# Decode attention with queries and probabilities as 32-column weights and the cache as the moving operand

## The chip, the cores and the metric

The kernel runs on one core of one Trainium2 chip. The metric is the device time of one execution in microseconds. Before the change it is 2065.58 us (median of 3 runs, 2065.29 to 2065.72).

The core has five engines that work side by side, each through its own instructions in order: TensorE (PE; its weight loads are listed apart as PEld), VectorE (DVE), ScalarE (ACT), GpSimd (POOL) and SyncE (SP), which here issues DMAs. TensorE multiplies a stationary operand (the weights, at most 128 rows by 128 columns) with a moving operand and writes to PSUM. The number of weight columns is the number of output partitions, and the number of moving columns is the length of the output.

## The reference

One layer of a hybrid decoder runs for a prompt of 256 tokens and for 8 decode sequences of one token each: a SwiGLU feed-forward half step, a mixing stage in which one half of the width is attention (16 query heads of 64, 4 key/value heads, window 128, a sink per head) and the other half an RWKV-7 recurrence, an output projection, a second SwiGLU, and norms. Everything is float32. The part in question is the attention of the decode tokens:

```python
def swa_decode(q, k, v, k_buf, v_buf, rel_bias, sinks):
    kc = jnp.concatenate([k_buf, k], axis=1)      # 128 cached keys and the token's own
    vc = jnp.concatenate([v_buf, v], axis=1)
    ...
    s = einsum('...qhgd,...khd->...hgqk', q, kc) * HEAD_DIM ** -0.5 + bias
    m = maximum(max(s), sink)
    p = exp(s - m);  denom = sum(p) + exp(sink - m)
    o = einsum('...hgqk,...khd->...qhgd', p / denom, vc)
```

So there are 8 sequences x 16 heads = 128 rows of 129 scores, and 128 output rows of 64. Each sequence has its own cache of 128 x 256 keys and as many values; a key/value head serves 4 query heads.

## The kernel before

**Layout and order.** All activations are held transposed: features on the partitions, and 264 columns for the 256 prompt tokens and the 8 decode tokens, so prompt and decode go through the large products together. Weights stream in chunks of 128 x 512: SP issues the load (tile `raw`), ACT rounds it to a high part (`hi`), VectorE takes the rest (`lo`), and each 128 x 128 piece costs three fast products (`gemm`, `chunk`, `mm`, line 73). The stages in time: first feed-forward, mixing from about 790 us, output projection from about 1160, second feed-forward from about 1300.

**Mixing as tasks.** `mixing_body` computes one tile of projected columns after another (`SEQ`: RWKV batches, then keys and values, then eight query tiles). What follows from a tile is a generator: `prep` and `chain` for RWKV, `kvtask` for keys and values, `attend` for one pair of query heads of the prompt, `dec_attend` for the decode tokens, `dec_state` for the RWKV state of the decode tokens. After every weight chunk `tick` lets each task go on to its next `yield`. That gives the order in the program; a planner with its own model of time then orders the instructions of each engine, and hands out buffers. Temporaries come from a pool of `NT` = 25 tiles (`tmp`, named `t` in the profile), loaded blocks from a ring of `NLD` = 6 (`load`, named `ld`), which bias, cached keys, cached values and state blocks share. A load waits on the SP queue until its buffer is free, and weight loads come behind it on that queue.

**Output projection.** It runs in three passes over the inner dimension (`PASS`): first the 8 RWKV tiles, then 6 attention tiles, then 2. The attention tasks run on during the first pass; the second needs them finished (`need`, `drain`), the decode part included: its results are copied into columns 256 to 263 of the attention tiles (line 813) and only then split into `hi` and `lo` (line 854).

**Decode attention before.** `attend` puts the 8 decode queries of its two heads into `qd` (line 708). `dec_attend` then

- spreads `qd` into `qb`, with zeros in the half of the partitions that belongs to the other head (line 756);
- for each of 2 pairs of key/value heads and 8 sequences loads the cached keys and multiplies with the keys as weights (128 x 128) and 8 query columns moving (line 765): 16 products, whose scores come out as positions by rows;
- copies the scores out, transposes them to rows by positions (line 773), computes the product with the token's own key separately (`pr` against `ones`), and adds bias, takes the softmax with the sink (`softmax`);
- transposes the probabilities back (line 787), spreads those of the token's own key with a diagonal matrix and a product with `ones`, and multiplies them with its own value on VectorE (`od`);
- multiplies the cached values as weights (128 x 128) with 8 probability columns moving: 16 products; adds them to `od`.

In the trace the 32 products with the cache are the rows `m<-t,ld`. Each float32 product is two instructions there.

Of the kernel before, what the change touches and what calls it, by code (L numbers as in the profile page):

```python
# [15 lines left out]
NB = 8  # L16
# [13 lines left out]
NS, NO, NH, NT, NLD = 45, 8, 40, 25, 6  # L30
# [13 lines left out]
CID, CBO, CCM, CTR, CMK = 0, 128, 256, 384, 512  # L44


def body(tc, I, O):
# [8 lines left out]
    def tt(e, out, a, b, op):  # L56
        return e.tensor_tensor(out=out, in0=a, in1=b, op=op)  # L57
# [36 lines left out]
    with ExitStack() as ctx:  # L94
# [48 lines left out]
        C = cp.tile([P, 640], F32, name="C")  # L143
# [146 lines left out]
        def mixing_body(mx, n2, n3):  # L290
            def fix(shape, name):
                return mx.tile(list(shape), F32, name=name)
# [4 lines left out]
            def load(src, shape):  # L297
                t = ring(shape, "ld", NLD)
                SP.dma_start(t, src)
                return t  # L300
# [16 lines left out]
            qd = fix((P, 2, NB, 4), "qd")  # L317
# [361 lines left out]
            def kvtask(w, p, x):  # L679
                A.dma_start(O[("kp", "vp")[w]][p], x[:, P:NP])  # L680
                yield
                tp = mp()
                TE.transpose(tp[0:8, 256:384], x[:, NP:T], ident)
# [21 lines left out]

            def attend(t, q):
                p = t // 4
                G.tensor_copy(qd[:, p, :, t % 4], q[:, NP:T])
# [41 lines left out]
            def dec_attend(att):  # L750
                yield
                qb = tmp((P, 2, NB, 2, 4))
                G.memset(qb, 0.0)
                for h in range(2):
                    r = HALF[h]
                    G.tensor_copy(qb[r, :, :, h, :], qd[r])
                yield
                sps = mp()
                sv = sps[:, :P].rearrange("p (h x) -> p h x", h=2)
                for p in range(2):  # L760
                    for b in range(0, NB, 2):
                        kc = load(I["kc"][p, b // 2], (P, 2, P))
                        for j in range(2):
                            c0 = p * 32 + (b + j) * 4
                            mm(sv[:, :, c0:c0 + 4], kc[:, j, :], qb[:, p, b + j])
                st = tmp((P, P))
                A.copy(st, sps[:, :P])
                pr = tmp((P, 2, NB, 4))
                for p in range(2):
                    tt(G, pr[:, p], qd[:, p], bc(kT[p][:, NP:T].unsqueeze(2), (P, NB, 4)), ALU.mult)  # L770
                yield
                s2 = mp()
                TE.transpose(s2[:, 0:P], st, ident)
                for h in range(2):
                    r = HALF[h]
                    mm(s2[r, P:P + 1], pr[r], ones[r, 0:1])
                bd = load(I["bd"], (P, 129))
                s = tmp((P, 129))
                mxv = ring((P, 2), "mxv", 6)
                V.tensor_tensor_reduce(out=s, in0=s2[:, 0:129], in1=bd, op0=ALU.add, op1=ALU.max, scale=1.0,  # L780
                                       scalar=vc(VSD), accum_out=mxv[:, 0:1])
# [6 lines left out]
                pt = tmp((P, P))  # L788
                A.copy(pt, tp[:, 0:P])
                pn = mp()  # L790
                for h in range(2):
                    r = HALF[h]
                    mm(pn[r, 0:64], ones[:, 0:64], dg[:, r])
                od = tmp((P, 2, NB, 4))
                for p in range(2):
# [4 lines left out]
                ov, pv = (x[:, :P].rearrange("p (h x) -> p h x", h=2) for x in (op, pt))  # L800
                for b in range(NB):
                    vcache = load(I["cv"][b], (P, 256))
                    for p in range(2):
                        c0 = p * 32 + b * 4
                        mm(ov[:, :, c0:c0 + 4], vcache[:, p * P:(p + 1) * P], pv[:, :, c0:c0 + 4])
                of = od.rearrange("p a b i -> p (a b i)")
                for h in range(2):
                    r = HALF[h]
                    tt(V, of[r], ov[r, h, :], of[r], ALU.add)
# [133 lines left out]
def layout(i):  # L943
# [3 lines left out]
    for n in (1, 2):  # L947
# [9 lines left out]
    heads = np.array([(2 * p + h) * 4 + j for h in range(2) for p in range(2) for b in range(NB) for j in range(4)])  # L957
# [9 lines left out]
                                 np.concatenate([m, m], 0)], 1).astype(f4))  # L967
# [46 lines left out]
```

## Time and profile before

| | |
|---|---|
| median of 3 runs | 2065.58 us |
| profiled execution, its own time | 2070.28 us |
| span of the profiled execution, first to last instruction | 2068.3 us |
| busy share PE / PEld / DVE / ACT / POOL | 97 / 95 / 63 / 51 / 14% |
| instructions | 45747 |
| mean granted TensorE clock | 0.99 |
| moved by DMA | 358.40 MB, mean 173 GB/s |

The profile is that of one execution. A row of the view by lines has the line of the kernel, the engine, the operation, what it writes and reads (buffer numbers left out), the shapes and the count; behind the bar stand the busy time in us, the mean time of one in ns, and the idle time of the engine before it with what ended it. Where a helper issues the instruction, its line is shown (73 for `mm`, 57 for `tt`), so the tile names tell the uses apart. A row of the timeline has start, length, engine, line, operation, tiles and count. A row of the view by stretches gives for each engine the busy time and, in brackets, the instructions. A row of the waits names the waiting engine and line, what it waited for, the time in total, how often, and the longest.

### The profile page before, as it was taken

To read this page: it belongs to the slowest core of one execution; us is meant where nothing else is said; L and a number is where in the kernel's file an instruction comes from. 1 tells how busy PE (TensorE), PEld (TensorE's weight loads), DVE (VectorE), ACT (ScalarE), POOL (GpSimd) and SP (SyncE) were. 2 spreads that over 40 slices of the span, in tenths; PEclk is the share of its full clock that TensorE was granted. 3 is DMA by queue.
4 is the path that set the end of the run, shared out by engine and by line. 5 is a ranking of instruction groups with operands and counts; after the bars stand their busy time and mean duration, and the time that the engine had idled before them with its cause. 6 is when DMAs were issued, how large, how long until landed. Compare 5 with 4: busy or idle time off the path is not lost.

```text
span 2068.3 us, 45747 instructions
## 1 busy us (share of the span) xinstructions
PE 2016.5 (97%) x17162; PEld 1973.1 (95%) x17162; DVE 1308.5 (63%) x2618; ACT 1056.2 (51%) x2080; POOL 287.9 (14%) x375
## 2 busy tenths in 40 slices
PE   8999999999999999989999899999999999999997
PEld 8999999999999999989998788999999999999997
DVE  5765555555555586668778788656555555655555
ACT  5644444444444466656565635544444444444445
POOL 0301001020110221211100052110101102010012
PEclk9999999999999999989999999999999999999998
DMA  6555565655555575443454465556555565555554
GB/s 225 176 177 185 175 206 177 195 179 176 186 174 188 181 217 188 140 121 104 143 144 129 125 183 180 177 181 181 181 175 186 169 193 181 179 182 176 185 174 139
DMA packets 228686, 358.40 MB, mean 173 GB/s; under 512 B 42304, under 2 KB 84304, under 8 KB 228432
## 3 DMA queue, kind: packets, MB, share of 16 engines
q1 hardware_dynamic: 222768, 346.82, 53.6%
q10 hardware_dynamic: 5696, 8.66, 1.1%
q8 instruction: 134, 2.20, 0.4%
q14 instruction: 88, 0.72, 0.1%
HBM read 347.25 MB, written 10.21 MB: 173 GB/s over the span
## 4 chain that ended last, share of the span: by engine, by line
PE 90%; DVE 4%; DMA 3%; issue 1%; ACT 1%; SPq 1%; POOL 0%; DVEq 0%; ACTq 0%; POOLq 0%
PE acc L73 82%; PE m L73 7%; DVE lo L57 1%; DMA raw<-in_gu 1%; DMA TT<-sb 1%; DMA sb<-Xt 1%; ACT L67 0%; DMA out_wkvs<-ld 0%; DVE s L60 0%; DVE s L57 0%; ACT t L67 0%; DVE ld L57 0%; DMA ld<-in_st 0%; SPq L509 0%; DVE y L57 0%
## 5 line engine op out<-in xcount | busy, mean ns | idle before, releaser
L73 PE MATMUL acc<-s,hi 128*128 128x264 f32 x6728 | 1257.8, 286 | 10.4 <-ACT hi L122 9.0
L57 DVE TENSOR_TENSOR lo<-raw,hi 128x512 fp32r<-128x512 f32 (+2 forms) x1304 | 877.3, 676 | 597.0 <-ACT hi L122 573.7
L122 ACT CAST hi<-raw 128x512 fp32r<-128x512 f32 (+2 forms) x1304 | 778.6, 602 | 880.2 <-PE acc L73 802.2
L73 PEld LDWEIGHTS acc<-s,hi 128*128 128x128 f32 x6728 | 1053.5, 190 | 18.4 <-ACT hi L122 10.3
L73 PE MATMUL acc<-s,lo 128*128 128x264 f32 x3364 | 964.3, 287 | 14.1 <-DVE lo L57 13.8
L73 PEld LDWEIGHTS acc<-s,lo 128*128 128x128 f32 x3364 | 636.0, 189 | 21.7 <-DVE lo L57 18.5
L73 PE MATMUL acc<-t,hi 128*128 128x264 f32 x2752 | 503.1, 285 | 1.6 <-ACT t L251 1.6
L73 PEld LDWEIGHTS acc<-t,hi 128*128 128x128 f32 x2752 | 426.1, 188 | 1.9 <-ACT t L251 1.8
L73 PE MATMUL acc<-t,lo 128*128 128x264 f32 x1376 | 388.5, 284 | 0.0
L57 POOL TENSOR_TENSOR t<-t,t 128x264 f32<-128x264 f32 (+1 forms) x146 | 156.8, 1074 | 1206.6 <-ACT hi L122 912.9
L73 PEld LDWEIGHTS acc<-t,lo 128*128 128x128 f32 x1376 | 258.3, 188 | 0.0
L57 DVE TENSOR_TENSOR t<-acc,t 128x264 f32<-128x264 f32 x164 | 70.9, 432 | 36.4 <-PE acc L73 36.1
L73 PE MATMUL acc<-o,hi 128*128 128x264 f32 x344 | 66.4, 284 | 0.0
L57 POOL TENSOR_TENSOR o<-o,o 128x264 f32<-128x264 f32 x48 | 40.7, 848 | 168.6 <-ACT o L67 166.2
L73 PEld LDWEIGHTS acc<-o,hi 128*128 128x128 f32 x344 | 53.3, 188 | 0.0
L67 ACT ACT_TABLE_LOAD x40 | 51.3, 1283 | 2.4 <-PEq L1006 1.2
L60 DVE SCALAR_TENSOR_TENSOR s<-acc,s 128x264 f32<-128x264 f32 x96 | 40.6, 427 | 16.8 <-PE acc L73 16.3
L73 PE MATMUL acc<-o,lo 128*128 128x264 f32 x172 | 49.1, 286 | 0.0
L60 DVE SCALAR_TENSOR_TENSOR x<-acc,x 128x264 f32<-128x264 f32 x96 | 40.5, 426 | 10.1 <-PE acc L73 9.7
L67 ACT ACTIVATE t<-t 128x264 f32<-128x264 f32 x94 | 40.0, 426 | 3.9 <-DVE t L57 2.4
L57 DVE TENSOR_TENSOR st<-X,Xt 128x60 f32<-128x60 f32 (+10 forms) x120 | 24.5, 204 | 22.3 <-DMA ld<-in_sT 9.7
L251 ACT CAST t<-t 128x264 fp32r<-128x264 f32 x86 | 35.5, 412 | 3.7 <-POOL t L57 2.3
(218 smaller groups left out, 1090.4 us busy)
## 6 DMA issues: line engine op xcount, KB each, us to landing
raw<-in_gu SPq DMA_DIRECT2D x688, 256.0 KB, 3.2
raw<-in_dn SPq DMA_DIRECT2D x224, 256.0 KB, 2.7
raw<-in_win SPq DMA_DIRECT2D x152, 256.0 KB, 3.3
raw<-in_dn SPq DMA_DIRECT2D x160, 192.0 KB, 2.7
raw<-in_wout SPq DMA_DIRECT2D x48, 256.0 KB, 3.5
raw<-in_wout SPq DMA_DIRECT2D x32, 128.0 KB, 2.5
xsp<-x ACTq DMA_DIRECT2D x16, 132.0 KB, 3.5
s<-xsp SPq DMA_DIRECT2D x16, 132.0 KB, 2.3
```

The lines of the kernel that those rows point to most:

```text
L57: return e.tensor_tensor(out=out, in0=a, in1=b, op=op)
L60: return V.scalar_tensor_tensor(out=out, in0=a, scalar=s, in1=b, op0=op0, op1=op1)
L67: return A.activation(out=out, in_=in_, func=f, **k)
L73: TE.matmul(out, lhsT, rhs, start=start, stop=stop, **k)
L122: A.copy(hi[:, :w], raw[:, :w])
L251: A.copy(hi, u)
```

## The change

The roles of the operands in the decode attention are exchanged. The queries, and later the probabilities, become weights of 32 columns, and the cached keys and values move.

- The 8 sequences are numbered b = 4u + g. Group g (0 to 3) gives the 32 columns of the array, and so the 32 partitions of the output, that its products use; within the group a row is (u, pair p, head h, query i).
- `QB` replaces `qd` and `qb`. It is zeroed once; `attend` writes its queries straight into it, with two copies of 64 partitions instead of one of 128. It has blocks of 8 columns at a distance of 40, so that any window of 32 columns that starts at 32 (2u + p) holds just one block, at its right place, and zeros.
- Scores: for each (p, u) two loads of keys and four products, one for each group, with a 32-column window of `QB` as weights and 128 positions moving. The four (p, u) accumulate into the same PSUM rows. They come out as rows by positions, so the copy and the first transposition go. The product with the own key takes `pr` as 128 columns of weights.
- Own value: the own-key probabilities are multiplied with a selection matrix (`CSL`, 8 more constant columns) and transposed to 8 x 128 (`own`); four products with the new values `vnew` (8 x 256), which `kvtask` now leaves in a tile of its own, start the accumulation.
- Values: the transposed probabilities are copied into `pz` with zeros beside them; for each u four loads of values and four products, 32 columns of weights, 256 value columns moving.
- The result is rows by value columns; it is copied out (`ao`), transposed in two halves, and four copies on ACT and VectorE take the needed blocks into `od`.
- The pool of temporaries goes from 25 to 21 tiles. The order of the rows of the bias and of the sinks (`heads`) follows the new order.

`dec_attend` has five `yield`s before its last part, as before; the products with the values lie one step earlier.

```diff
-NS, NO, NH, NT, NLD = 45, 8, 40, 25, 6
+NS, NO, NH, NT, NLD = 45, 8, 40, 21, 6
...
-            qd = fix((P, 2, NB, 4), "qd")
+            QB = fix((P, 4, 160), "QB")
+            G.memset(QB, 0.0)
+            qv = QB.rearrange("p g (c x) -> p g c x", x=40)
+            vnew = fix((NB, 256), "vnew")
...
-                    kvn[w] = tmp((8, 256))
+                    kvn[w] = vnew if w else tmp((NB, 256))
...
-                G.tensor_copy(qd[:, p, :, t % 4], q[:, NP:T])
+                for h in range(2):
+                    G.tensor_copy(qv[HALF[h], :, p:4:2, h * 4 + t % 4], gu(q[HALF[h], NP:T]))
...
+                pr, pz = tmp((P, 4, 4, 8)), tmp((P, 4, 2, 32))
+                G.memset(pz, 0.0)
+                for p in range(2):
+                    tt(G, pr[:, :, p:4:2, :], qv[:, :, p:4:2, 0:8],
+                       bc(gu(kT[p][:, NP:T]).unsqueeze(3), (P, 4, 2, 8)), ALU.mult)
                 yield
                 sps = mp()
-                        kc = load(I["kc"][p, b // 2], (P, 2, P))
-                            mm(sv[:, :, c0:c0 + 4], kc[:, j, :], qb[:, p, b + j])
+                mm(sps[:, P:P + 1], pr.rearrange("p g c x -> p (g c x)"), ones[:, 0:1])
                 for p in range(2):
+                    for u in range(2):
+                        kc = [load(I["kc"][p, 2 * u + j], (P, 2, P)) for j in range(2)]
+                        for g in range(4):
+                            c0 = (2 * u + p) * 32
+                            mm(sps[g * 32:g * 32 + 32, 0:P], QB[:, g, c0:c0 + 32], kc[g // 2][:, g % 2, :],
+                               p + u == 0, p + u == 2)
...
-                dg = tmp((P, P))
-                ts(V, dg, ident, s[:, P:P + 1], ALU.mult)
+                ts(V, t8, C[:, CSL:CSL + NB], s[:, P:P + 1], ALU.mult)
                 yield
                 tp = mp()
                 TE.transpose(tp[:, 0:P], s[:, 0:P], ident)
+                TE.transpose(tp[0:NB, P:2 * P], t8, ident)
+                own = tmp((NB, P))
+                for u in range(2):
+                    A.copy(pz[:, :, u, u * 16:u * 16 + 16],
+                           tp[:, 0:P].rearrange("p (g u x) -> p g u x", g=4, u=2)[:, :, u, :])
+                A.copy(own, tp[0:NB, P:2 * P])
+                yield
+                av = mp()
+                for g in range(4):
+                    mm(av[g * 32:g * 32 + 32, 0:256], own[:, g * 32:g * 32 + 32], vnew, True, False)
+                for u in range(2):
+                    vcache = [load(I["cv"][4 * u + g], (P, 256)) for g in range(4)]
+                    for g in range(4):
+                        mm(av[g * 32:g * 32 + 32, 0:256], pz[:, g, u, :], vcache[g], False, u == 1)
+                ao = tmp((P, 256))
+                A.copy(ao, av[:, 0:256])
+                yield
+                op = mp()
                 for p in range(2):
-                    tt(V, od[:, p], pn[:, p * 32:p * 32 + 32].rearrange("p (b i) -> p b i", i=4),
-                       bc(vT[p][:, NP:T].unsqueeze(2), (P, NB, 4)), ALU.mult)
+                    TE.transpose(op[:, p * P:(p + 1) * P], ao[:, p * P:(p + 1) * P], ident)
+                od = tmp((P, 2, 2, 4, 4))
...
+                        (A.copy, V.tensor_copy)[h](od[HALF[h], p].rearrange("p u g i -> p g u i"),
+                                                   ov[HALF[h], p, :, :, x:x + 4])
```

More of the change, by code (lines that the diff above doesn't have):

```diff
@@ L766, in dec_attend @@
[L766 to L776, printed above, removed]
+                    for u in range(2):
[4 more added lines that the diff above has]
+                               p + u == 0, p + u == 2)
@@ L787, in dec_attend @@
                 TE.transpose(tp[:, 0:P], s[:, 0:P], ident)
[L788 to L795, printed above, removed]
-                    tt(V, od[:, p], pn[:, p * 32:p * 32 + 32].rearrange("p (b i) -> p b i", i=4),
-                       bc(vT[p][:, NP:T].unsqueeze(2), (P, NB, 4)), ALU.mult)
+                TE.transpose(tp[0:NB, P:2 * P], t8, ident)
@@ L798, in dec_attend @@
+                ao = tmp((P, 256))
+                A.copy(ao, av[:, 0:256])
                 yield
                 op = mp()
[L800 to L806, printed above, removed]
@@ L807, in dec_attend @@
-                for h in range(2):
-                    r = HALF[h]
-                    tt(V, of[r], ov[r, h, :], of[r], ALU.add)
+                for p in range(2):
+                    TE.transpose(op[:, p * P:(p + 1) * P], ao[:, p * P:(p + 1) * P], ident)
+                od = tmp((P, 2, 2, 4, 4))
+                ov = op[:, 0:256].rearrange("p (q g u x) -> p q g u x", q=2, g=4, u=2)
+                for p in range(2):
+                    for h in range(2):
+                        x = p * 8 + h * 4
+                        (A.copy, V.tensor_copy)[h](od[HALF[h], p].rearrange("p u g i -> p g u i"),
+                                                   ov[HALF[h], p, :, :, x:x + 4])
@@ L956, in layout @@
     sc = cols[:NSH * P] - 1536
-    heads = np.array([(2 * p + h) * 4 + j for h in range(2) for p in range(2) for b in range(NB) for j in range(4)])
+    heads = np.array([(2 * p + h) * 4 + j for g in range(4) for u in range(2) for p in range(2) for h in range(2)
+                      for j in range(4)])
     a["vec"] = c(np.concatenate([
```

23 lines of the change are left out of this document (9 added, 14 removed).

## The prediction

> **What bounds the kernel now.** I read the page first: which engine is full, and where it is not.
>
> ```profile
> span 2068.3 us, 45747 instructions
> PE 2016.5 (97%) x17162; PEld 1973.1 (95%) x17162; DVE 1308.5 (63%) x2618; ACT 1056.2 (51%) x2080; POOL 287.9 (14%) x375
> PE 90%; DVE 4%; DMA 3%; issue 1%; ACT 1%; SPq 1%; POOL 0%; DVEq 0%; ACTq 0%; POOLq 0%
> ```
>
> TensorE is busy for 97% of the span and carries 90% of the chain that ended last. So time taken off PE is worth its full length wherever PE is the late one, and nothing where another engine is. The change sits in one place, from the first load of cached keys at 1172.4 us to the last product with cached values, which ends at 1220.9:
>
> ```profile
> L299 SPq DMA_DIRECT2D ld<-in_kc x8: 328/342/524, 1172.4 to 1193.5; - x8
> 1198.59 0.95 PE L73 MATMUL m<-t,ld 128*128 128x8 f32 x8
> 1211.30 1.84 PE L73 MATMUL m<-t,ld 128*128 128x8 f32 x16
> 1219.81 1.06 PE L73 MATMUL m<-t,ld 128*128 128x8 f32 x8 [0.61 <-DMA ld<-in_cv]
> ```
>
> I read that neighbourhood in stretches (columns: length, then PE, PEld, DVE, ACT, POOL, clock, DMA).
>
> ```profile
> 1190.00:1200.00 10.00, 10.00 (x77) 8.81 (x77) 6.10 (x21) 4.01 (x14) 1.68 (x4) 1.00 0.56 161
> 1200.00:1210.00 10.00, 10.00 (x87) 9.61 (x86) 8.59 (x25) 4.48 (x10) 3.74 (x4) 1.00 0.72 205
> 1210.00:1220.00 10.00, 9.31 (x68) 7.67 (x66) 9.40 (x16) 2.97 (x6) 9.50 (x14) 1.00 0.70 218
> 1225.00:1230.00 5.00, 5.00 (x40) 4.69 (x39) 4.97 (x11) 3.86 (x10) 5.00 (x10) 1.00 0.28 87
> 1230.00:1235.00 5.00, 2.62 (x20) 2.19 (x19) 5.00 (x7) 1.24 (x2) 5.00 (x6) 1.00 0.74 215
> 1245.00:1250.00 5.00, 4.48 (x36) 4.34 (x36) 5.00 (x11) 2.05 (x4) 3.29 (x3) 1.00 0.53 170
> 1250.00:1260.00 10.00, 10.00 (x84) 10.00 (x84) 6.86 (x16) 4.30 (x9) 0.47 (x1) 1.00 0.75 228
> ```
>
> Up to 1210 PE is full and VectorE is not. From 1225 to 1250 VectorE is full (4.97 and 5.00 of 5) and PE is not: 2.62 of 5 just after 1230. The chain of waits says where it changes over:
>
> ```profile
> 1202.64 1.84 PE acc L73 x14
> 1204.48 3.50 issue
> 1209.13 4.60 DMA out_wkvs<-ld
> 1213.75 2.04 DMA ld<-in_cv
> 1217.04 3.83 DMA ld<-in_st
> 1245.62 31.23 PE acc L73 x255
> ```
>
> Until 1204.5 the late thing is PE. From there to 1245.6 it is the ring of six `ld` buffers (a cached-value load waits until a state block has been stored out of its buffer) and then VectorE with `dec_state` and the splits; PE is late again only from 1245.6. The old score products (K, the burst at 1198.59 is the last) end before 1200, the old value products (V) lie behind 1211.3. So K is on the path, V is beside it.
>
> **The change part by part.** Durations from the lines, shapes kept apart, and one use of each kind in time:
>
> ```profile
> L73 PE MATMUL m<-t,ld 128*128 128x8 f32 x64 | 7.8, 250 | 0.7 <-DMA ld<-in_cv 0.6
> L73 PE MATMUL m<-t,s 128*64 128x256 f32 x32 | 9.1, 437 | 0.0
> L73 PE MATMUL m<-t,s 128*64 128x128 f32 x32 | 5.7, 299 | 0.0
> L73 PE MATMUL m<-t,ones 128*64 128x64 f32 x4 | 0.3, 246 | 0.0
> L73 PE MATMUL m<-ones,t 64*64 64x1 f32 x4 | 0.3, 204 | 0.0
> L683 PE MATMUL m<-C,s 128*8 128x128 f32 x3 | 0.8, 273 | 0.0
> L773 PE MATMUL m<-C,t 128*128 128x128 f32 x1 | 0.3, 272 | 0.0
> PEld m L73 <- issue: 6.1, 27, 0.4
> PEld acc L73 <- issue: 5.9, 20, 0.7
> 1209.32 0.34 PE L73 MATMUL m<-t,ones 128*64 128x64 f32 x4
> ```
>
> Each float32 product is two instructions in the trace (32 products, 64 rows). The two waits of PEld for "issue", between 780 and 1330 us, stand where the array is cut differently from the instruction before: 12.0 us over 47 times, 0.255 each. I price every entry into narrow weights and every return at that.
>
> K, removed: 16 products of 128x128 keys as weights, 32 instructions of 7.8/64 = 0.122: 3.9 us. The transposition of the scores (L773, 0.3) and the product with `ones` (0.3, with two changes of cut, 0.5) go as well. Together 5.0.
> K, added: 16 products with 32 columns of weights and 128 columns moving, in four column groups. A 128-column instruction of narrow weights costs 5.7/32 = 0.178. One after another, 32 make 5.7; four abreast 1.4. The trace has no four abreast. It has two: the four `ones` instructions of two 64-column groups are over in 0.34, with a mean of 0.246 each, so they overlap. I take four abreast, 1.4, since that row shows groups over the same 128 rows running together, and keep 5.7. Two bursts, four changes of cut: 1.0 (four bursts 2.0). The own-key product becomes two full instructions, 0.24. Together 2.6. K side: 2.6 - 5.0 = -2.4 us.
>
> V, removed: 32 instructions again, 3.9, the 0.7 that they waited for loads, and the broadcast of own probabilities (0.3, and two changes, 0.5). Together 5.4. V, added: 4 own-value and 8 cached products with 256 columns moving, 24 instructions of 9.1/32 = 0.284: 6.8 in a row, 1.7 abreast; two bursts, 1.0; an 8-wide transposition (0.8/3 = 0.27) and two full ones (0.56). Together 3.5. V side: -1.9 us.
>
> The Trainium skill, "TensorE: Matmul & The Clock Gate", Part 3, gives three column tiles a measured speedup of 2.38, 0.79 for each; carried on to four (an estimate from that page) it is 3.2 where I use 4, K + V would be 12.5/3.2 = 3.9 instead of 3.1, and my forecast would be 0.4 us later. No run here shows four.
>
> Beside PE: the query copies double (8 to 16 on POOL), `QB` is cleared once (five times the 128 columns of the `ones` memset) and `pz` once.
>
> ```profile
> L708 POOL COPY qd<-q x8: 197/200/710, 1065.1 to 1152.7; 128x8 f32<-128x8 f32 x8
> L146 POOL MEMSET ones<- x1: 205/205/205, 0.7 to 0.7; 128x128 f32 x1
> POOL qd L708 <- DVE q L60: 86.9, 8, 18.8
> ```
>
> That is 8 x 0.2 + 5 x 0.2 + 2 x 0.2 = 3 us of POOL, which sat 86.9 us waiting for queries in just this stage; taken at nothing, 3 us if POOL were late. ACT gets six small copies for two and is under half busy in every stretch above but one (3.86 of 5); VectorE loses the diagonal scaling and four adds and gets two copies, under 1 us less. The extra POOL copy comes in front of the bias work of its own head only. DMAs: the same eight key, eight value and one bias load, no byte more, but keys are held two at a time and values four at a time out of six buffers.
>
> Fewer temporaries, 25 to 21 (they pay for `QB`): no row prices it. The use of them shows in one place:
>
> ```profile
> 1212.06 8.40 POOL L57 TENSOR_TENSOR t<-XR 128x256 f32<-128x256 f32 x11
> 1214.18 6.57 DVE L57 TENSOR_TENSOR t<-XR 128x256 f32<-128x256 f32 x9
> 1223.89 0.45 DVE L57 TENSOR_TENSOR t<-m,t 64x64 f32<-64x64 f32 x2
> 1224.40 3.07 POOL L813 COPY o<-t 128x8 f32<-128x8 f32 x8 [3.94 <-DVE t L57]
> PE m L73 <- DVE gm L57: 5.2, 1, 5.2
> L673 SPq DMA_DIRECT2D out_wkvs<-ld x16: 343/344/438, 1190.6 to 1250.9; - x16
> ```
>
> `dec_state` runs ahead there and fills twenty tiles (11 on POOL, 9 on VectorE) before it can use them. With 21 it runs ahead by four fewer; the gain of that is at most 4/20 of the 6.57, -1.3 us. At the other end a preparation of `prep` comes late and PE waits as it did for `gm`, +5.2. I take nothing: what the run-ahead does early is not wanted early.
>
> **The sum.** K side -2.4 arrives, since the chain is PE's there. V side -1.9 lies between 1204.5 and 1245.6, where the chain is not PE's; I count nothing. The profiled execution took 2070.28 us (its span and 2.0 around it), 4.7 over the median of the runs, 2065.58. 2070.3 - 2.4 = 2067.9 against that execution; against the median 2063.2, -0.12%.
>
> **The rivals.**
> Faster: the V side arrives too. For it: a value load waited for a buffer (the 2.04 and 4.60 of the chain), and the new order asks for values one step of the task earlier, so the ring can turn earlier and `dec_attend` ends before 1224. Against it: VectorE is full from 1225 to 1250. Time: 2065.6 - 4.3 = 2061.3, with the 1.3 of the shorter run-ahead 2060.0, and 2057.6 if the 2.4 that PE stood after 1230 goes too.
> Slower: the output of the decode attention finds no buffer. `ao` and `od` are taken after the V products; if `dec_state` holds the pool by then (it filled twenty by 1220.8, and there are 21 now), each waits until one of its blocks is through. The sixteen blocks were stored from 1190.6 to 1250.9, 3.8 us each; two waits are 7.5 us, and all of it is on the path, because the eight copies (3.07) and the splits of the second output pass come behind it and PE already starves there (2.62 of 5). Time: 2065.6 - 2.4 + 7.5 = 2070.7; one wait alone 2067, and with the 5.2 of a late `prep` on top of two 2076. It decides once fewer than two buffers are free when V ends.
> Not what it says: the groups do not run together. Then K side is 5.7 + 0.24 + 2.0 - 5.0 = +2.9 and V side 6.8 + 0.83 + 1.5 - 5.4 = +3.7; 2068.5 if V stays covered, 2072.2 if not. Against it is the 0.34 row. In the Trainium skill, the same page and part, a weight load overlaps a running product only if their row groups differ; the four groups here share all rows, so by that rule this rival would hold. The 0.34 row speaks against the rule.
>
> **How the numbers follow.** Likeliest, 0.44: 2063.2, own range 2061.5 to 2066. Faster rival 0.27: 2061.3 down to 2057.6. No buffer 0.20. Not together 0.09. About 0.2% (4.1 us) is what can be told from no change, so 2061.4 and 2069.7 divide: faster 0.27, within 0.44 and slower 0.29, of which a part of the slow rivals' lower end would still count as no change. The range, 2057.5 to 2074, leaves out about a tenth at either end.
>
> **What would show it.** K: 32 instructions with 32-column weights in about 1.4 us of PE; four starts within a few ns, then a gap of one stream. V: 24, about 1.7. The 64 rows of 128x8 are gone. PE should stay full to about 1202 and every later event come 2 to 3 us sooner; after 1225 VectorE should still be full. Wrong if starts of the groups follow one another by a whole stream; if the copies into the mixed rows (3.07 of POOL) begin later than 1224.4; if PE's idle time between 890 and 1060 grows (too few temporaries); if the stretch after 1230 gains more than K gave (ring freed sooner).

## The result, and the profile after

The changed kernel takes 2075.25 us (median of 6 runs, 2072.43 to 2075.81), beside 2065.65 us for the kernel before on the same chip. The ratio is 1.0036, with a 95% interval of 1.0026 to 1.0046: it is slower by 7.4 us (0.0036 x 2065.65). The two medians are 9.6 us apart, the upper end of that interval; from here on the text goes by ratios. The profiled execution took 2075.56 us and has a span of 2073.5 us. The page of the profile after:

```profile
span 2073.5 us, 45734 instructions
PE 2019.3 (97%) x17150; PEld 1972.2 (95%) x17150; DVE 1309.1 (63%) x2616; ACT 1056.6 (51%) x2084; POOL 289.7 (14%) x382
```

The shares of the engines over the whole span have not moved. So the place has to be found in time. I cut out the stretch from the last store of the RWKV state (`wkvp`) to the first weight load of the second feed-forward. In the view by stretches (columns as in the prediction) it is, in before and then in after:

```profile
1149.30:1286.60 137.30, 125.79 (x942) 112.29 (x940) 112.46 (x280) 71.63 (x179) 45.17 (x61) 0.98 0.56 170
```

```profile
1145.70:1290.10 144.40, 128.89 (x930) 111.19 (x928) 113.27 (x278) 72.31 (x183) 43.37 (x60) 0.94 0.54 161
```

After was 3.6 us ahead at the start of this stretch and 3.5 us behind at its end. It is 7.1 us longer, more than the 5.2 us between the two spans (2073.5 and 2068.3). TensorE stood idle for 4 us more there (144.40 - 128.89 against 137.30 - 125.79) and was busy for 3.1 us more, and its granted clock fell from 0.98 to 0.94. Smaller pieces show when, first before, then after:

```profile
1190.00:1230.00 40.00, 39.30 (x305) 35.78 (x304) 34.02 (x82) 16.68 (x42) 20.98 (x32) 1.00 0.59 175
1205.00:1219.00 14.00, 13.91 (x108) 12.27 (x106) 12.67 (x27) 4.45 (x11) 10.38 (x14) 1.00 0.68 206
1230.00:1270.00 40.00, 36.08 (x287) 34.92 (x286) 33.41 (x66) 16.18 (x32) 13.45 (x14) 1.00 0.69 217
```

```profile
1190.00:1230.00 40.00, 38.14 (x285) 31.09 (x284) 28.73 (x64) 16.73 (x41) 13.49 (x19) 1.00 0.59 176
1205.00:1219.00 14.00, 13.94 (x106) 10.68 (x105) 6.85 (x14) 4.55 (x9) 1.76 (x2) 1.00 0.66 191
1230.00:1270.00 40.00, 33.23 (x231) 32.22 (x232) 35.21 (x67) 13.70 (x29) 17.51 (x23) 0.87 0.62 186
```

The middle rows carry the case. From 1205 to 1219 VectorE worked 12.67 us before and 6.85 us after, and GpSimd 10.38 and 1.76. That work did not vanish: it came later, when the output of the decode attention needed the same two engines. After 1230 TensorE then has 33.23 us of work in 40 instead of 36.08, at a clock of 0.87 instead of 1.00. The timeline of after names the work, first on GpSimd (start, length, line, what it writes and reads, count; in square brackets the idle time before):

```profile
1220.03 1.18 POOL L57 TENSOR_TENSOR ld<-ld,t 128x256 f32<-128x256 f32 x1 [12.47 <-PE m L742]
1221.17 6.91 POOL L57 TENSOR_TENSOR t<-XR 128x256 f32<-128x256 f32 x9
1228.03 1.39 POOL L815 COPY o<-t 128x8 f32<-128x8 f32 x4
1232.00 1.39 POOL L815 COPY o<-t 128x8 f32<-128x8 f32 x4
1234.05 0.92 POOL L57 TENSOR_TENSOR s<-o,s 128x264 fp32r<-128x264 f32 x1
```

then on VectorE and ScalarE:

```profile
1215.18 0.42 DVE L57 TENSOR_TENSOR ld<-ld,XR 128x256 f32<-128x256 f32 x1 [3.21 <-DMA ld<-in_st]
1219.39 0.42 DVE L57 TENSOR_TENSOR ld<-ld,t 128x256 f32<-128x256 f32 x1
1224.05 0.20 DVE L809 COPY t<-m 64x32 f32<-64x32 f32 x1
1224.49 3.87 DVE L57 TENSOR_TENSOR t<-XR 128x256 f32<-128x256 f32 x5
1228.62 1.08 DVE L57 TENSOR_TENSOR t<-XR 128x256 f32<-128x256 f32 x3
1229.73 0.20 DVE L809 COPY t<-m 64x32 f32<-64x32 f32 x1
1230.38 1.21 DVE L57 TENSOR_TENSOR lo<-raw,hi 128x512 fp32r<-128x512 f32 x1
1224.28 0.18 ACT L809 COPY t<-m 64x32 f32<-64x32 f32 x1 [4.18 <-DVE t L809]
1224.37 1.14 ACT L122 CAST hi<-raw 128x512 fp32r<-128x512 f32 x2
```

`t<-XR` are the multiplications of `dec_state` that need no state block; before, nine on VectorE and eleven on GpSimd ran from 1212 to 1221, while the attention waited for values (rows in the prediction). In after GpSimd stood still for 12.47 us, because its queue had an addition into a state block (`ld<-ld,t`) ahead of them, and then did nine of them in front of the copies into the mixed rows (L815). That block was there by 1215.18, when VectorE began on it; the addition also needs VectorE's subtraction, which came at 1219.39. (The releaser in the row's brackets is inferred by the profile.) On VectorE eight stand between the first and the last copy out of the turned output (L809). The four L809 copies wait for one another through `od`, so ScalarE, which also casts the weights, waited 4.18 us. The first copy into the mixed rows began at 1228.03 (1224.40 before), the first split (`s<-o,s`) on GpSimd at 1234.05 (1228.14 before). That split and the longest stop of TensorE between 1230 and 1270, in before:

```profile
1228.14 1.19 POOL L57 TENSOR_TENSOR s<-o,s 128x264 fp32r<-128x264 f32 x1
1231.69 0.39 PE L73 MATMUL acc<-s,lo 128*128 128x264 f32 x1 [1.41 <-DVE lo L57]
```

TensorE in after:

```profile
1231.64 0.49 PE L73 MATMUL acc<-s,lo 128*128 128x264 f32 x1 [3.43 <-DVE lo L57]
1231.92 0.64 PE L73 MATMUL acc<-s,hi 128*128 128x264 f32 x2
1235.80 0.40 PE L73 MATMUL acc<-s,hi 128*128 128x264 f32 x2
1243.00 0.59 PE L73 MATMUL acc<-s,lo 128*128 128x264 f32 x1 [4.02 <-DVE lo L57]
1243.39 0.64 PE L73 MATMUL acc<-s,hi 128*128 128x264 f32 x2
```

It stands for 3.43 and 4.02 us, and behind each stop the same pair of products takes 0.64 instead of 0.40 us: the granted clock is halved there. In before the longest stop between 1230 and 1270 was 1.41 us, and the clock stayed at 1.00. In the Trainium skill, "TensorE: Matmul & The Clock Gate", Part 1, an idle window of about 3.4 us halves the clock; these two stops agree. A shorter stop was enough in e15, one of the runs below, where 1.84 us were followed by a clock of 0.50 (the stop, then the stretch behind it):

```profile
1251.74 0.39 PE L73 MATMUL acc<-s,lo 128*128 128x264 f32 x1 [1.84 <-DVE lo L57]
1253.00:1255.00 2.00, 2.00 (x12) 2.00 (x10) 2.00 (x4) 0.62 (x1) 1.06 (x1) 0.50 0.89 257
```

Both stops of after are waits for `lo`, the low part of a weight chunk, which VectorE makes. By the order of the casts, the one that VectorE made at 1230.38 belongs to a chunk that ScalarE had rounded before 1225.6 (L122 above); it stood behind the copies and the multiplications. At the first stop no split of the decode attention's output had run yet (the first came at 1234.05), and the products right behind the stop need none. So the moved work reached TensorE on two ways: through the late output, and straight through VectorE's queue, in which the weights' `lo` stand too.

### The profile page after: what moved, and what is told of

Same layout as the page of the kernel before. It is cut to its first block, busy times and chain, and to the rows that moved or that the text cites. A ratio compares the mean times of both kernels' runs of the same rounds, so it can differ in the third digit from the quotient of the medians.

```text
span 2073.5 us, 45734 instructions
## 1 busy us (share of the span) xinstructions
PE 2019.3 (97%) x17150; PEld 1972.2 (95%) x17150; DVE 1309.1 (63%) x2616; ACT 1056.6 (51%) x2084; POOL 289.7 (14%) x382
## 5 line engine op out<-in xcount | busy, mean ns | idle before, releaser
L122 ACT CAST hi<-raw 128x512 fp32r<-128x512 f32 (+2 forms) x1304 | 779.0, 602 | 891.0 <-PE acc L73 815.1
L73 PE MATMUL acc<-s,lo 128*128 128x264 f32 x3364 | 965.9, 288 | 17.5 <-DVE lo L57 17.3
```

The source lines that it names most:

```text
L73: TE.matmul(out, lhsT, rhs, start=start, stop=stop, **k)
L122: A.copy(hi[:, :w], raw[:, :w])
```

## The experiments

**The first theory and its rivals.** I began with the four L809 copies as the cause (theory "copies"). Rivals were the smaller pool, and the V side's own tail: more steps, and values that are held four at a time. Each ratio below is against runs of the kernel before on the same chip, with its 95% interval.

**e1, the pool alone.**

```diff
-NS, NO, NH, NT, NLD = 45, 8, 40, 25, 6
+NS, NO, NH, NT, NLD = 45, 8, 40, 21, 6
```

> The kernel before with one number changed: 21 temporary slots in the mixing in place of 25; the decode attention keeps its old form. Theory 'copies' (the four alternating ScalarE and VectorE copies of the turned output queue behind the state update, and the second output pass starts late): the pool is no cause, so the time stays within 2 us of before, 2063.5 to 2067.5, or falls by up to 3 us as the trace of after was 3.5 us ahead at 1156. Rival 'pool' (four slots fewer lengthen the mixing): 2072 to 2077, the whole loss or most of it.

Measured: 0.9999 (0.9990 to 1.0008). The pool is no cause.

**e2, the copies on ScalarE.**

```diff
-                        (A.copy, V.tensor_copy)[h](od[HALF[h], p].rearrange("p u g i -> p g u i"),
+                        A.copy(od[HALF[h], p].rearrange("p u g i -> p g u i"),
```

> The kernel after with all four copies of the turned output on ScalarE, none on VectorE. Theory 'copies': they then end about 1220 in place of 1230, the first copy into the mixed rows starts by 1225, the three idle stretches of TensorE after 1231 shrink to those of before, and the time comes out 6 to 9 us under after, 2066 to 2069. Rival 'pool' or rival 'values' (the value loads one by one are what makes it late): within 2 us of after, 2073 to 2077.

Measured: 1.0036 (1.0024 to 1.0049). The theory fell. GpSimd in e2 shows why:

```profile
1222.78 2.19 POOL L815 COPY o<-t 128x8 f32<-128x8 f32 x8
1224.94 5.38 POOL L57 TENSOR_TENSOR t<-XR 128x256 f32<-128x256 f32 x7
1230.28 0.92 POOL L57 TENSOR_TENSOR s<-o,s 128x264 fp32r<-128x264 f32 x1
```

The copies are early now, even against before, but the multiplications then stand in front of the splits. The queue has moved by one place.

**e3 and e4, one side turned back.** e3 has keys as weights again, with the copy and the transposition of the scores (and one `yield` more). e4 has values as weights again, with the own value by a broadcast, and no `pz`, `own` and `ao`.

> The kernel after with the K side in the old roles: keys as weights, eight query columns moving, a copy and a transpose of the scores behind them; the V side and the pool as in after. Theory 'copies': the cause is in the V side's tail, so the loss stays, 2073 to 2079 (the K side's own gain of some 2 us given back). If the K side of the change costs time, 2065 to 2070. Rival 'pool': 2072 to 2078.

> The kernel after with the V side in the old roles: values as weights, eight probability columns moving, the own value by a broadcast product on VectorE (four products in place of two of before, as the groups order the columns otherwise), two additions at the end; the K side and the pool as in after. Theory 'copies': the loss goes, 2063 to 2067. Rival 'pool': it stays, 2072 to 2077.

Measured: e3 1.0025 (1.0017 to 1.0034), e4 0.9991 (0.9982 to 0.9999). The loss is tied to the V side. From e4 to after it is 1.0036 - 0.9991, 0.45% or 9.3 us. e4 keeps the K side and the small pool and is 1.9 us under before. In e4 GpSimd does its multiplications while the values are on their way, ahead of the copies (L813 in this kernel):

```profile
1208.91 5.22 POOL L57 TENSOR_TENSOR t<-XR 128x256 f32<-128x256 f32 x7
1221.52 2.60 POOL L813 COPY o<-t 128x8 f32<-128x8 f32 x8
```

**e5 to e8, the order of the state update.** The second theory was "run-ahead": multiplications that run ahead of their blocks get in the way. e5 (after), e6 (e4's form) and e7 (before) forbid the running ahead, by the same mark on all five operations of a step:

```diff
-                    tt(G, t1, bc(XR[:, 3, r].unsqueeze(2), shp), bj(4), ALU.mult)
-                    tt(V, S, S, bj(1), ALU.mult)
+                    keep = tc.keep_in_program_order
+                    keep(tt(G, t1, bc(XR[:, 3, r].unsqueeze(2), shp), bj(4), ALU.mult))
+                    keep(tt(V, S, S, bj(1), ALU.mult))
...
```

e8 starts the update of after one output pass later.

```diff
-                if pi == 0:
+                if pi == 1:
                     dst = spawn(dec_state())
```

> The kernel after with the five operations of each state-update step kept in program order from step to step, so that the multiplications that need no state block cannot be queued ahead on VectorE and GpSimd; nothing else is changed. Theory 'run-ahead' (these multiplications stand in both queues in front of the turned output, its copies and the splits of the second output pass, and the later V tail of after meets them): the splits start by 1226 and end by 1233, and the time falls by 6 to 11 us against after, to a ratio of 0.995 to 0.999 to before. Rival 'V tail' (the values' own later end alone makes the pass late): the ratio stays 1.002 to 1.004.

> The K side of the change with the V side in the old roles, and the state update's operations kept in program order. Theory 'run-ahead': little remains to be gained by the V side's form, so within 0.1% of the ordered after: 0.995 to 0.999 of before. Rival 'V tail': some 0.4% under the ordered after, 0.995 to 0.998 of before, while the ordered after stays over 1.002.

> The kernel before with the state update's operations kept in program order, nothing else changed. Theory 'run-ahead': the five idle stretches of TensorE between 1230 and 1246 in before, 3.9 us together, are of the same cause and shrink, 0.997 to 0.999 of before; the ordered after then lies 0 to 3 us under this one, the K side's gain. Rival: the order costs as much as it gives, 0.999 to 1.002.

> The kernel after with the state update begun only with the second output pass, behind its drain, in place of the first: while the decode attention runs nothing of the update is in any queue, and its loads are not in the ring of six. Theory 'run-ahead': the values arrive earlier and the output of the attention is ready by 1222; the loss goes unless the update then collides with the third pass, 0.996 to 1.001 of before. Rival 'V tail': the loss stays at 1.002 to 1.004, as the tail itself is as long.

Measured: e5 1.0022 (1.0013 to 1.0032), e6 0.9993 (0.9983 to 1.0002), e7 1.0008 (0.9998 to 1.0019), e8 1.0034 (1.0024 to 1.0045). By the numbers set beforehand this theory fell too: e5 gave back 3 us, not 6 to 11, and e8 nothing. In e8 the output was split early, but eleven multiplications of the update then met the weights of the second pass:

```profile
1228.95 8.39 POOL L57 TENSOR_TENSOR t<-XR 128x256 f32<-128x256 f32 x11 [4.21 <-ACT XR L659]
```

So I took the run-ahead as not bad in itself. It is work that has to be done somewhere, and there is one stretch in which it costs nothing, the one where after had both engines idle. That gave the third theory, "state": the V side costs nothing by itself, it only moves the update out of that stretch.

**e9 to e11, without the state update.** The update is left out, with its loads, its stores and the products that turn its columns, and the state is copied through by one transfer, in after (e9), in e4's form (e10) and in before (e11).

```diff
                 while any(g.left for g in bts):
                     yield
-                ps = mp()
...
-                    SP.dma_start(O["wkvs"][:, r, :], S)
+                A.dma_start(O["wkvs"], I["st"])
                 yield
```

> The kernel after without the arithmetic of the state update: the state is copied to the output by one transfer on ScalarE's queue, and its five turned columns, its 80 operations, its loads and its stores are left out. Theory 'state' (the turned V side by itself costs nothing; it only moves the time at which the state update's VectorE and GpSimd work falls): within 2 us of the V-back kernel without the update, and 0 to 4 us under before without it. Rival 'V tail': 4 to 9 us over the V-back kernel without the update.

> The K side of the change with the V side in the old roles, without the arithmetic of the state update (as in the run before this one). Both theories: 1 to 4 us under before without the update, by the K side's gain; 5 to 14 us under before with it, as the idle stretches of TensorE after 1230 go.

> The kernel before without the arithmetic of the state update. The base of the other two: 4 to 12 us under before.

Measured, all against before with its update: e9 0.9956 (0.9941 to 0.9971), e10 0.9969 (0.9960 to 0.9978), e11 0.9984 (0.9974 to 0.9993). Without the update the whole change is faster: 0.28% or 5.8 us from e11 to e9, their intervals just apart (e9 has four runs). Some 3 us of it lie between e11 and e10, the K side, and some 3 between e10 and e9, the V side; the intervals overlap in both of these pairs. The rival "V tail" wanted e9 4 to 9 us over e10, and it falls; theory "state" wanted no more than 2 us between these two, and it was 2.7. With the update the V side costs 9.3. Read the other way, leaving the update out takes 3.3 us off before (4 to 12 were expected), 4.5 off e4's form and 16.5 off after (1.0036 - 0.9956). The cause is thus the two together, and neither alone.

**e12, the multiplications ahead.** The whole change is kept, with its pool and its turned V side. From the fourth step of the update on, the multiplications are issued six steps ahead, in program order.

```diff
+                    while len(pre) <= k + (6 if k >= 3 else 0) and len(pre) < 64 // n:
+                        rr = slice(len(pre) * n, len(pre) * n + n)
+                        t1, t2 = tmp(shp), tmp(shp)
+                        keep(tt(G, t1, bc(XR[:, 3, rr].unsqueeze(2), shp), bj(4), ALU.mult))
+                        keep(tt(V, t2, bc(XR[:, 0, rr].unsqueeze(2), shp), bj(2), ALU.mult))
+                        pre.append((t1, t2))
...
-                    t1, t2 = tmp(shp), tmp(shp)
+                    t1, t2 = pre[k]
```

> The kernel after with the state update's operations in program order, and the multiplications that need no state block issued six steps ahead from the fourth step on, so that on GpSimd seven of them stand before the addition that waits for the fourth block, where VectorE and GpSimd were idle in after from 1207 to 1218. Theory 'state': a ratio of 0.999 to 1.002 to before, under that of after and of the ordered after. Rival 'V tail': 1.002 to 1.004, as both of those.

Measured: 0.9995 (0.9985 to 1.0005). The order of this work alone takes 0.41%, 8.5 us, off the changed kernel, the whole of its loss; program order without the six steps (e5) had taken 3. The timeline of e12:

```profile
1205.75 5.00 POOL L57 TENSOR_TENSOR t<-XR 128x256 f32<-128x256 f32 x7
1214.72 2.43 DVE L57 TENSOR_TENSOR t<-XR 128x256 f32<-128x256 f32 x7
1219.52 0.83 POOL L820 COPY o<-t 128x8 f32<-128x8 f32 x4 [8.77 <-DVE t L814]
```

and its stretch after 1230, where the clock is whole again:

```profile
1230.00:1270.00 40.00, 36.45 (x286) 34.86 (x285) 34.53 (x77) 15.60 (x32) 13.98 (x14) 1.00 0.66 201
```

**e13 to e15, the same elsewhere.** e13 is e12's edit on e4's form, e14 on before. e15 is after with eight steps ahead from the third step on, and e2's edit.

> The K side of the change with the V side in the old roles, and the state update's multiplications issued six steps ahead in program order, as in the run on after. Interplay: no gain over the V-back kernel, whose multiplications already ran in that stretch: 0.998 to 1.001 of before, and the same form with the turned V side (0.9995) within 0.1% of it. If the reordering helps any form: 0.991 to 0.996.

> The kernel before with the state update's multiplications issued six steps ahead in program order. Interplay: no gain, 0.999 to 1.002 (keeping the update in order alone gave 1.0008). If the reordering helps any form: 0.992 to 0.997.

> The kernel after with the state update's multiplications issued eight steps ahead from the third step on, and the four copies of the turned output on ScalarE, so that none of them waits in VectorE's queue. Interplay: under the run with six ahead, 0.997 to 0.9995 of before. If the order of the queues has given all it can: 0.9985 to 1.001.

Measured: e13 0.9984 (0.9973 to 0.9994), e14 0.9992 (0.9980 to 1.0003), e15 1.0016 (1.0006 to 1.0027). The edit gives 0.07% and 0.08% to the two old V sides, which is within the intervals, and 0.41% to the new one, as "interplay" expected; that e12 lies within 0.1% of e13 was missed by a little (0.11%). e13, the K side of the change with the old V side and the reordered update, is the best of all that keep the update, 3.3 us under before. e15 missed: earlier is not better. The third addition into a state block then ran at 1219.3, the blocks kept their places in the ring of six, and the last value load was issued at 1218.6 (1210.6 in e12).

**e16, a ring for the state blocks.** As e12, with state blocks in a ring `sd` of two of their own, and 20 temporaries.

> The kernel after with the state update's multiplications six steps ahead, and the state blocks loaded into a ring of their own of two in place of the ring of six shared with keys and values (20 temporary slots). If the shared ring holds back the values: the last value load is issued by 1206 in place of 1210.6, and the ratio to before is 0.996 to 0.999. If it does not: 0.999 to 1.002, as with six ahead alone (0.9995).

Measured: 1.0015 (1.0005 to 1.0024). The last value load came earlier, at 1207.5, as the theory of the shared ring wanted, and the kernel became slower all the same: with two blocks at a time the update lasted until 1275 (1265.9 in e12), beside the second pass.

**e17 and e18, which addition blocks.** In the order of GpSimd's instructions, before and e4 have as many additions ahead of the long row of multiplications as state blocks are loaded ahead of the values (four and three). After and e3 have one more. The loads in before, then in after (`in_st` are state blocks, `in_cv` values):

```profile
1197.39 1.49 SPq L299 DMA_DIRECT2D ld<-in_st  x2
1199.46 0.37 SPq L299 DMA_DIRECT2D ld<-in_cv  x1
```

```profile
1211.03 0.90 SPq L299 DMA_DIRECT2D ld<-in_cv  x2
1212.02 1.33 SPq L299 DMA_DIRECT2D ld<-in_st  x3
```

The fourth block comes ahead of the values in before and behind the last of them in after, and its addition waited until 1220.03. e17 adds a `yield` ahead of the value products:

```diff
                 yield
+                yield
                 av = mp()
```

e18 has this too, and takes away the one behind them:

```diff
                 A.copy(ao, av[:, 0:256])
-                yield
```

With either, four blocks are loaded ahead of the values; five additions stand ahead of the multiplications in e17 and four in e18.

> The kernel after with one more yield ahead of the value products. Four state blocks are then loaded ahead of the values, but five additions stand ahead of the ten multiplications in GpSimd's queue, so one still waits for a block behind the values. Theory 'blocked addition': the multiplications run on GpSimd after 1218 as in after, and the loss stays, 1.002 to 1.006. Rival 'values too early' (the loss comes of the value loads standing ahead of the fourth block): 0.998 to 1.001.

> The kernel after with the yield behind the value products moved ahead of them; as many yields as in after. Four state blocks are loaded ahead of the values, and four additions stand ahead of the nine multiplications in GpSimd's queue. Theory 'blocked addition': the multiplications run on GpSimd from about 1209 on and the loss goes or halves (VectorE's own still stand behind its subtractions), 0.9985 to 1.002. Rival 'V tail' or any cause that the turned V side carries with it: 1.003 to 1.006.

Measured: e17 1.0027 (1.0016 to 1.0039), e18 1.0034 (1.0022 to 1.0045). e17 kept its loss, as the blocked addition says. e18 is a miss. GpSimd is freed as foreseen:

```profile
1208.13 4.82 POOL L57 TENSOR_TENSOR t<-XR 128x256 f32<-128x256 f32 x6
1229.22 1.72 POOL L815 COPY o<-t 128x8 f32<-128x8 f32 x4 [1.24 <-DVE t L809]
```

but VectorE's multiplications still ran from 1223 to 1229, between the copies out of the output, and the copies into the mixed rows waited for those. Freeing GpSimd alone is not enough, nor (e2) is taking the copies off VectorE; e12 does it for both engines.

**All runs in one measure.** For each kernel: from the end of the last value product to the end of the sixth split in order of time, whichever tiles those are (the second pass takes six), both read from the timeline of its profiled execution.

| kernel | last value product | sixth split | us between | ratio |
|---|---|---|---|---|
| before | 1220.9 | 1235.5 | 14.6 | 1 |
| e1, pool | 1220.7 | 1236.5 | 15.8 | 0.9999 |
| e4, V back | 1216.7 | 1233.6 | 16.9 | 0.9991 |
| e6, V back, ordered | 1214.1 | 1224.1 | 10.0 | 0.9993 |
| e7, before, ordered | 1216.0 | 1227.9 | 11.9 | 1.0008 |
| e12, after, ahead | 1215.3 | 1230.0 | 14.7 | 0.9995 |
| e13, V back, ahead | 1215.9 | 1228.3 | 12.4 | 0.9984 |
| e14, before, ahead | 1216.5 | 1227.7 | 11.2 | 0.9992 |
| e15, after, ahead 8 | 1223.6 | 1240.1 | 16.5 | 1.0016 |
| e16, after, own ring | 1212.4 | 1227.7 | 15.3 | 1.0015 |
| e5, after, ordered | 1214.1 | 1231.4 | 17.3 | 1.0022 |
| after | 1216.2 | 1241.8 | 25.6 | 1.0036 |
| e2, copies on ScalarE | 1217.9 | 1239.7 | 21.8 | 1.0036 |
| e3, K back | 1219.3 | 1242.5 | 23.2 | 1.0025 |
| e17 | 1220.4 | 1245.3 | 24.9 | 1.0027 |
| e18 | 1217.9 | 1240.2 | 22.3 | 1.0034 |

Five kernels need 21.8 us or more, and all five lose 0.25% or more. No kernel with the old V side needs more than 16.9. The three between, e5, e15 and e16, split in time or nearly so and still lose 0.15 to 0.22%. In e5, TensorE has no long stop but fifteen short ones for `lo`, 9.2 us in all (6.8 in e6): there the update's work lies in the second pass. Left out of the table are e8, which splits early (10.8) and pays in the same pass, and the three without the update (8.9 to 10.8).

The stretch from the last store of the RWKV state to the first weight load of the second feed-forward sorts the runs without looking at the splits, and takes in e8. It is 143.2 to 146.1 us long in after, e2, e3, e8, e17 and e18, which lose 0.25% or more, 140.5 to 142.9 in e5, e7, e15 and e16, and 137.5 to 140.0 in e1, e4, e6, e12, e13 and e14 (137.3 in before).

**What stays open.** Why the planner put one addition more ahead of the multiplications in after, I did not find out. Which engine's part weighs more was not separated: no run frees VectorE alone. Nor was it separated how much came through the late output and how much straight through the weights' `lo`; what the traces show is that TensorE's stops of over 1 us between 1230 and 1275 all wait for VectorE, in every run. And the second feed-forward, from its first weight load to its last product, took 767 to 772 us in the twenty profiled executions of the same code, after 770.2 beside 768.6 before; that is part of every difference between two traces here, and no run explains it.

## Why the prediction was wrong, point by point

Predicted were 2063.2 us and a range to 2074; measured 2075.25.

- **K side, -2.4.** Borne out by e4, at -1.9 us (0.9991, interval 0.2 to 3.7 us), and by e11 to e10, at -3 with intervals that overlap. From e3 to after, with the V side turned in both, it goes the other way, +2.3 (1.0025 to 1.0036, overlapping too), so the gain is not shown beside the new V side. The score products of after are:

```profile
L73 PE MATMUL m<-ld,QB 128*32 128x128 f32 x32 | 2.3, 283 | 0.0
1187.22 0.63 PE L73 MATMUL m<-ld,QB 128*32 128x128 f32 x12
```

  The groups run abreast (twelve instructions in 0.63 us, of which one alone was priced at 0.178), but in five bursts, not two, so 2.3 us and not 1.4. The 0.5 that I added to each burst for its two changes of cut was too much: by the starts in the timeline the five bursts with their changes took 2.6 us, and the sum had 1.4 and 1.0. The two errors cancel, which is luck. The reduction over the scores with the bias began 6.3 us sooner, 1196.90 against 1203.23. Of this, 3.4 were there when the first keys were loaded (1168.98 against 1172.41), so they are no gain of the score products.

- **V side, -1.9, counted as nothing.** This is the step that failed. With the state update in the kernel it costs 9.3 us (e4 to after). The products themselves are no gain:

```profile
L73 PE MATMUL m<-ld,t 128*32 128x256 f32 x16 | 3.1, 391 | 0.1
1207.74 0.64 PE L73 MATMUL m<-ld,t 128*32 128x256 f32 x8
1209.16 0.62 PE L73 MATMUL m<-ld,t 128*32 128x256 f32 x2
```

  Eight instructions of four groups take 0.64 us and the two of one group take 0.62. The last four values arrived one by one, so they paid the full stream four times over. I had priced two bursts. But that is 2 us of TensorE in all; the V side had ended 4.7 us before its time in before (1216.2 against 1220.9). The loss lies in what it did to the queues of the other engines: I asked whether the V side is on the path, and not what work of the update stands in its waits.

- **"What the run-ahead does early is not wanted early."** This sentence of mine is what the runs refute. I used it to price four temporaries fewer at nothing, and in that it held (e1). But the run-ahead filled the one stretch in which VectorE and GpSimd were free. Where it leaves that stretch, it comes back in front of the output and of the weights' `lo`. I had the row of it (eleven multiplications on GpSimd, nine on VectorE, from 1212 to 1221), and did not ask what the change does to their place.

- **"ACT gets six small copies for two", at nothing; VectorE "gets two copies, under 1 us less".** The work is as small as said, 0.2 us a copy. I named the cover, half a free ScalarE, but not what they would stand behind: VectorE's first copy ran only at 1224.05, and ScalarE waited 4.18 us for it, with the casts of the weights behind it; VectorE's second copy stood behind five and three multiplications. That these copies alone are not the cause, e2 shows.

- **The rival "slower: no buffer"** had 2070.7 to 2076 with the right place and about the right size, but another mechanism, so that it comes near is luck. No wait for a buffer shows at `ao` (L799) or `od` (L809): `ao` was copied out 0.04 us after the last value product had ended (1215.53 + 0.62), and `od` 0.04 us after its transpositions (1218.99 + 0.38). In after:

```profile
1215.53 0.62 PE L73 MATMUL m<-ld,t 128*32 128x256 f32 x2
1216.19 0.37 ACT L799 COPY t<-m 128x256 f32<-128x256 f32 x1 [1.16 <-PE m L73]
1218.99 0.38 PE L803 MATMUL m<-C,t 128*128 128x128 f32 x2
1219.41 0.18 ACT L809 COPY t<-m 64x32 f32<-64x32 f32 x1
```

  What was short was the time of two engines.

- **The granted clock** was not in my sum. Two stops of 3.4 and 4 us on TensorE brought about 10 us at half clock (13% of the 40 us after 1230 are missing from the clock), up to 5 us of work on top of the stops.

- **The tests I named.** "The copies into the mixed rows begin later than 1224.4" came true (1228.03), and was the sign of the error. TensorE's idle time between 890 and 1060 did not grow: it was 6.9 us in after and 7.5 before (170 less 163.06 and 162.55 busy).

- **The rival "not together"** was wrong, as the bursts show, and with it the rule in the Trainium skill ("TensorE: Matmul & The Clock Gate", Part 3) that a weight load overlaps running products only across row groups: all four groups here have all 128 rows.

## What to carry to other kernels

An engine that waits inside a stage is often doing another stage's work there. Before moving or shortening a stage, list what the planner has put into its waits and ask where that work goes, on each engine's in-order queue; an instruction that waits holds everything free that stands behind it (12.47 us of GpSimd here). When a stage gets shorter and the kernel slower, take the neighbouring task away in both versions: three runs without the state update separated the parts here, after several edits at the symptom had not.

## What the runs showed of the hardware

**VectorE and GpSimd slow each other.** Multiplications of the same kind (128 x 256, `t<-XR`) took 0.35 us each on VectorE in e12, where GpSimd was idle (seven in 2.43, from 1214.72), and 0.77 each in after, where GpSimd did the same at that time (five in 3.87, from 1224.49). GpSimd's began 0.57 us apart in e12 while VectorE stood still (from 1206.84 to 1208.55), and took 0.77 each in after (nine in 6.91). So on VectorE the moved work took twice the length that it has alone; in before, where the two ran side by side as well, it was 0.73 (nine in 6.57). The Trainium skill, "SBUF — State Buffer", section "SBUF: two separate sides", has the two engines lock a shared pair of ports for a whole instruction where VectorE has two inputs. The rows show that the two slow each other; that one stands for the whole of the other's instruction they do not, as 0.35 and 0.57 in turn would make 0.92 for one of each, and it was 0.77.

**Four column groups with full rows run abreast**, eight instructions of 256 columns in 0.64 us, and the two of a lone product take 0.62: a burst with three groups missing is as long as a full one.
